# An 8192 x 8192 fp32 transpose re-tiled: two strips of 4096 columns, staggered 1024-row regions, one DMA queue

## The chip, the cores and the metric

The kernel runs on one core of one Trainium2 chip; the chip's other cores are idle. The metric is the device time of one execution in microseconds (us). All times below are medians of several executions, all of them fast. A ratio is the mean time of one kernel's fast runs over that of the other's of the same rounds, so not quite the ratio of the medians that are quoted. One caution: the profiled execution is a single one. For the kernel before it took 1276.94 us, 1.5 us more than its median.

## The reference

```python
x = np.random.randn(8192, 8192).astype(np.float32)
def reference(x):
    return np.transpose(x)
```

268.4 MB must be read and 268.4 MB written. TensorE transposes blocks of 128 x 128 from SBUF to PSUM, ScalarE (ACT) and VectorE (DVE) copy them to SBUF, and DMAs do the rest.

## The kernel before

The input is cut into 32 blocks of 1024 rows x 2048 columns. A block is loaded by two DMAs of 4 MB (packets of 8 KB, one row's piece), then transposed in 16 groups of 8 blocks of 128 x 128; each group is copied by ACT or DVE in turn, and after four groups ACT issues a store of 2 MB (4 KB contiguous in DRAM, 16 KB contiguous in SBUF). Loads go through SP's queue, stores through ACT's.

```python
R = 8; C = 16; I = R * P; J = C * P       # block: 1024 rows, 2048 columns
G = 4; LS = 2; NIN = 2; NOUT = 4; NPS = 4
# ... cut: allocation, semaphores, identity
for k, (bi, bj) in enumerate(blocks):
    # ... cut
    if k >= NIN:
        nc.sync.wait_ge(s_pe, (k - NIN + 1) * C)
    for s in range(LS):
        src = x[i0 + s * rs * P:i0 + (s + 1) * rs * P, j0:j0 + J]
        nc.sync.dma_start(out=in_tile[:, s * rs:(s + 1) * rs, :],
            in_=src.rearrange("(a p) j -> p a j", p=P)).then_inc(s_ld[slot][s], 16)
    for g in range(C // G):
        for bb in range(G):
            # ... cut: 8 transposes into one PSUM tile, a copy by ACT or DVE
        dst = out[j0 + g * G * P:j0 + (g + 1) * G * P, i0:i0 + I]
        # ... cut: ACT waits for the four copies
        if ng < NG:
            st = wide_dma(nc, nc.scalar, "qActDynamicHW", dst, outs[ob])
```

Note that the transposes of a group span all 1024 rows: no store can start before a whole block has landed.

Of the kernel before, what the change touches and what calls it, by code (L numbers as in the profile page):

```python
# [1 line left out]

# [5 lines left out]


def physical(ap):  # L10


    t = ap.tensor
    dims = [list(d) for d in ap.ap]
    if len(dims) == 2:
        dims.insert(1, [dims[1][1], 1])
    return mybir.PhysicalAccessPattern(
        ap=dims,
        offset=ap.offset,
        dtype=ap.dtype,  # L20
        memref=t.name,
        memsetref=t.name + "_set",
    )


def wide_dma(nc, eng, queue, out, in_):


    return eng.add_instruction(  # L29
        mybir.InstDMACopy(  # L30
            mode="Copy",
            name=nc.get_next_instruction_name(),
            engine=eng.engine,
            ins=[physical(in_)],
            outs=[physical(out)],
            queue=queue,
        )
    )


@with_exitstack
def kernel(
    ctx: ExitStack,
    tc: tile.TileContext,
    x: bass.AP,
    out: bass.AP,
):
    nc = tc.nc
    P = 128
    N, M = x.shape  # L50
    assert x.shape == out.shape[::-1]
    dt = x.dtype

    R = 8
    C = 16
    I = R * P
    J = C * P
    G = 4
    LS = 2
    NIN = 2  # L60
    NOUT = 4
    NPS = 4

    with tc.tile_critical():  # L64
        nc.alloc_sbuf_tensor("pad", [P, 32], dt)
        ident = nc.alloc_sbuf_tensor("ident", [P, P], dt).ap()
        ins = [nc.alloc_sbuf_tensor(f"in_tile{k}", [P, R, J], dt).ap() for k in range(NIN)]
        outs = [nc.alloc_sbuf_tensor(f"out_tile{k}", [P, G * I], dt).ap() for k in range(NOUT)]
        pss = [nc.alloc_psum_tensor(f"ps{k}", [P, I], dt).ap() for k in range(NPS)]

        s_id = nc.alloc_semaphore("s_id")
        s_ld = [[nc.alloc_semaphore(f"s_ld{k}_{s}") for s in range(LS)] for k in range(NIN)]
        s_st = [nc.alloc_semaphore(f"s_st{k}") for k in range(NOUT)]
        s_pe = nc.alloc_semaphore("s_pe")
        s_cp = [nc.alloc_semaphore("s_cpa"), nc.alloc_semaphore("s_cpv")]

        nc.gpsimd.memset(ident, 0.0).then_inc(s_id, 1)  # L77
        nc.gpsimd.wait_ge(s_id, 1)
        nc.gpsimd.affine_select(  # L79
            out=ident,  # L80
            in_=ident,
            compare_op=mybir.AluOpType.not_equal,
            fill=1.0,
            base=0,
            pattern=[[-1, P]],
            channel_multiplier=1,
        ).then_inc(s_id, 1)
        nc.tensor.wait_ge(s_id, 2)

        blocks = [(bi, bj) for bj in range(M // J) for bi in range(N // I)]  # L90
        rs = R // LS
        n = 0
        ng = 0
        NG = len(blocks) * (C // G)
        for k, (bi, bj) in enumerate(blocks):
            slot, use = k % NIN, k // NIN
            i0, j0 = bi * I, bj * J
            in_tile = ins[slot]


            if k >= NIN:
                nc.sync.wait_ge(s_pe, (k - NIN + 1) * C)
            for s in range(LS):
                src = x[i0 + s * rs * P:i0 + (s + 1) * rs * P, j0:j0 + J]
                nc.sync.dma_start(  # L105
                    out=in_tile[:, s * rs:(s + 1) * rs, :],
                    in_=src.rearrange("(a p) j -> p a j", p=P),
                ).then_inc(s_ld[slot][s], 16)
            for g in range(C // G):
                ob, ouse = ng % NOUT, ng // NOUT  # L110
                ng += 1
                for bb in range(G):
                    b = g * G + bb
                    ps = pss[n % NPS]
                    e = n % 2
                    eng = (nc.scalar, nc.vector)[e]
                    if n >= NPS:
                        nc.tensor.wait_ge(s_cp[(n - NPS) % 2], (n - NPS) // 2 + 1)
                    for a in range(R):
                        if b == 0 and a % rs == 0:  # L120
                            nc.tensor.wait_ge(s_ld[slot][a // rs], 16 * (use + 1))
                        ins_t = nc.tensor.transpose(  # L122
                            ps[:, a * P:(a + 1) * P],
                            in_tile[:, a, b * P:(b + 1) * P],
                            ident,
                        )
                    ins_t.then_inc(s_pe, 1)
                    eng.wait_ge(s_pe, n + 1)
                    if bb < 2 and ouse > 0:
                        eng.wait_ge(s_st[ob], 16 * ouse)  # L130
                    o = outs[ob][:, bb * I:(bb + 1) * I]
                    if e == 0:
                        c = nc.scalar.copy(out=o, in_=ps)  # L133
                    else:
                        c = nc.vector.tensor_copy(out=o, in_=ps)  # L135
                    c.then_inc(s_cp[e], 1)
                    n += 1
                dst = out[j0 + g * G * P:j0 + (g + 1) * G * P, i0:i0 + I]
                nc.scalar.wait_ge(s_cp[0], n // 2)
                nc.scalar.wait_ge(s_cp[1], n // 2)  # L140
                dst = dst.rearrange("(b q) i -> q b i", q=P)
                if ng < NG:
                    st = wide_dma(nc, nc.scalar, "qActDynamicHW", dst, outs[ob])
                else:
                    st = nc.scalar.dma_start(out=dst, in_=outs[ob])
                st.then_inc(s_st[ob], 16)
        for ob in range(NOUT):
            nc.sync.wait_ge(s_st[ob], 16 * (ng // NOUT))


# [1 line left out]
_INS = ['x']  # L152
_OUTS = [((8192, 8192), 'float32')]


# [23 lines left out]
```

## Time and profile before

| | before |
|---|---|
| time | 1275.41 us (1275.17 to 1275.65, 3 runs) |
| bytes moved by the kernel | 536.9 MB |
| rate between the edges (slices 3 to 38 of 40) | 425 to 430 GB/s, one slice 421 |
| load packet of 8 KB / store packet of 16 KB, most frequent duration | 309 / 615 ns |

From the page of the kernel before: the busy time of PE, the mean busy share of the 16 DMA engines in tenths in 40 slices of 31.9 us each, what they moved, and the two queues (q1 loads, q10 stores: packets, MB, share of 16 engines' time).

```profile
PE 524.8 (41%) x4096; PEld 513.3 (40%) x4096; DVE 313.5 (25%) x256; ACT 251.3 (20%) x257; POOL 0.7 (0%) x6
...
DMA  9999999999999999999999999999999999999996
GB/s 393 417 430 426 426 427 428 428 430 426 429 425 428 429 427 430 426 426 430 427 427 429 427 429 425 428 421 426 429 427 428 425 426 429 428 427 428 427 398 269
...
q1 hardware_dynamic: 33792, 268.44, 49.9%
q10 hardware_dynamic: 18816, 268.44, 49.6%
```

The DMA engines are full in all slices but the last; PE is busy for 41%. The view of waits (engine and line, what it waited for: us in total, times, longest) says the same from the other side: everybody waits for loads.

```profile
ACT out_tile L133 <- PE ps L122: 1007.6, 160, 29.6
DVE out_tile L135 <- PE ps L122: 947.2, 256, 30.4
PE ps L122 <- DMA in_tile<-in_x_dram: 734.1, 43, 26.2
```

The windows view shows the edges. Columns: the window in us, its length, busy us of each engine (with instructions), granted TensorE clock, mean busy share of the DMA engines, GB/s.

```profile
core 0: us, PE busy (x) PEld busy (x) DVE busy (x) ACT busy (x) POOL busy (x), PEclk, DMA share, GB/s
5.00:28.00 23.00, 6.39 (x40) 6.02 (x41) 1.89 (x2) 2.02 (x2) 0.00 (x0) 1.00 1.01 429
1212.00:1230.00 18.00, 10.39 (x96) 10.15 (x93) 8.09 (x7) 5.79 (x6) 0.00 (x0) 0.91 1.02 432
1230.00:1244.00 14.00, 0.00 (x0) 0.00 (x0) 0.00 (x0) 0.00 (x0) 0.00 (x0) 0.50 0.79 336
1244.00:1250.00 6.00, 5.99 (x40) 5.99 (x41) 2.26 (x2) 2.03 (x2) 0.00 (x0) 0.72 0.05 19
1250.00:1254.00 4.00, 4.00 (x39) 4.00 (x37) 2.63 (x3) 1.93 (x2) 0.00 (x0) 1.00 0.70 299
1254.00:1258.00 4.00, 4.00 (x39) 4.00 (x38) 2.76 (x3) 2.02 (x3) 0.00 (x0) 1.00 0.99 414
1272.00:1275.00 3.00, 0.00 (x0) 0.00 (x0) 0.00 (x0) 0.00 (x0) 0.00 (x0) 0.50 0.02 10
```

The first line is the start, in which only the load queue runs: one queue alone streams at about 429 GB/s. From 1230 us on, the stream falls apart: the last loads land at different times on different engines, then the last block must be transposed, and until the first of its four stores is under way the engines stand idle. In the records of the single DMA packets I counted, for each us, how much of 16 busy engines is missing. For this tail the sum is **9.9 us of full stream**. In the middle of it lie 4.9 us (4.87) in which no data packet at all is in flight. I call the first the hole's mean area, the second the standstill of all engines.

### The profile page before, as it was taken

To read this page: it belongs to the slowest core of one execution; us is meant where nothing else is said; L and a number is where in the kernel's file an instruction comes from. 1 tells how busy PE (TensorE), PEld (TensorE's weight loads), DVE (VectorE), ACT (ScalarE), POOL (GpSimd) and SP (SyncE) were. 2 spreads that over 40 slices of the span, in tenths; PEclk is the share of its full clock that TensorE was granted. 3 is DMA by queue.
4 is the path that set the end of the run, shared out by engine and by line. 5 is a ranking of instruction groups with operands and counts; after the bars stand their busy time and mean duration, and the time that the engine had idled before them with its cause. 6 is when DMAs were issued, how large, how long until landed. Compare 5 with 4: busy or idle time off the path is not lost.

```text
span 1275.1 us, 9369 instructions
## 1 busy us (share of the span) xinstructions
PE 524.8 (41%) x4096; PEld 513.3 (40%) x4096; DVE 313.5 (25%) x256; ACT 251.3 (20%) x257; POOL 0.7 (0%) x6
## 2 busy tenths in 40 slices
PE   3245523345333553425544154431454324544134
PEld 3244523345332553425544154431454314444134
DVE  1133312233112331213322133211333113332023
ACT  1122211222111221212212022211222112221112
POOL 0000000000000000000000000000000000000000
PEclk9677756777667776667766677666777667776677
DMA  9999999999999999999999999999999999999996
GB/s 393 417 430 426 426 427 428 428 430 426 429 425 428 429 427 430 426 426 430 427 427 429 427 429 425 428 421 426 429 427 428 425 426 429 428 427 428 427 398 269
DMA packets 52648, 537.47 MB, mean 421 GB/s; under 512 B 3072, under 2 KB 3072, under 8 KB 3584
## 3 DMA queue, kind: packets, MB, share of 16 engines
q1 hardware_dynamic: 33792, 268.44, 49.9%
q10 hardware_dynamic: 18816, 268.44, 49.6%
q8 instruction: 32, 0.52, 0.2%
q14 instruction: 8, 0.07, 0.0%
HBM read 268.44 MB, written 268.44 MB: 421 GB/s over the span
## 4 chain that ended last, share of the span: by engine, by line
another core or an unknown queue 39%; DMA 32%; PE 28%; issue 0%; DVE 0%; ACT 0%; ACTq 0%; SPq 0%
DMA in_tile<-in_x_dram 32%; PE ps L122 28%; DVE out_tile L135 0%; ACT out_tile L133 0%; ACTq L29 0%; SPq L105 0%; SPq L174 0%; ACTq L130 0%; ACTq L140 0%; SPq L64 0%
## 5 line engine op out<-in xcount | busy, mean ns | idle before, releaser
L122 PE MATMUL ps<-ident,in_tile 128*128 128x128 f32 x4096 | 524.8, 296 | 734.6 <-DMA in_tile<-in_x_dram 734.1
L122 PEld LDWEIGHTS ps<-ident,in_tile 128*128 128x128 f32 x4096 | 513.3, 155 | 745.8 <-DMA in_tile<-in_x_dram 702.4
L135 DVE COPY out_tile<-ps 128x1024 f32<-128x1024 f32 x256 | 313.5, 1225 | 947.2 <-PE ps L122 947.2
L133 ACT COPY out_tile<-ps 128x1024 f32<-128x1024 f32 x256 | 250.0, 1016 | 1007.6 <-PE ps L122 1007.6
L133 ACT ACT_TABLE_LOAD x1 | 1.3, 1283 | 0.9 <-SPq L64 0.9
L79 POOL TENSOR_SCALAR_AFFINE_SELECT ident<-ident 128x128 f32<-128x128 f32 x1 | 0.3, 294 | 0.2 <-POOL ident L77 0.2
L77 POOL MEMSET ident<- 128x128 f32 x1 | 0.2, 206 | 0.5 <-SPq L64 0.5
L163 POOL MEMSET const-bfloat16-1.0<- 128x1 bf16 x1 | 0.1, 102 | 0.0
L163 POOL MEMSET const-uint8-127<- 128x1 uint8 x1 | 0.1, 102 | 0.0
L163 POOL MEMSET const-float32-0.0<- 128x1 f32 x1 | 0.1, 99 | 0.2 <-issue 0.2
L163 POOL MEMSET const-float32-1.0<- 128x1 f32 x1 | 0.1, 99 | 0.0
## 6 DMA issues: line engine op xcount, KB each, us to landing
in_tile<-in_x_dram SPq DMA_DIRECT2D x64, 4096.0 KB, 39.3
out_dram<-out_tile ACTq DMA_DIRECT2D x128, 2048.0 KB, 17.6
```

The lines of the kernel that those rows point to most:

```text
L77: nc.gpsimd.memset(ident, 0.0).then_inc(s_id, 1)
L79: nc.gpsimd.affine_select(out=ident, in_=ident, compare_op=mybir.AluOpType.not_equal, fill=1.0, base=0, pattern=[[-1, P]], channel_multipl ...
L122: ins_t = nc.tensor.transpose(ps[:, a * P:(a + 1) * P], in_tile[:, a, b * P:(b + 1) * P], ident,)
L133: c = nc.scalar.copy(out=o, in_=ps)
L135: c = nc.vector.tensor_copy(out=o, in_=ps)
L163: nc = _bacc.Bacc("TRN2", target_bir_lowering=False, num_devices=1)
```

## The change

The intent: smaller steps, so that the stream never waits for a block. A strip is 4096 columns wide and is read in chunks of 128 rows (2 MB, packets of 16 KB). Its eight column ranges of 512 columns each fill a region of their own; each region takes 1024 rows, but the regions are staggered, so that one of the eight is complete and stored after each chunk. At both ends of a strip the regions are shorter (a staircase of 1 to 7 chunks). SP issues loads and stores, in one queue. The copies become half as wide and twice as many.

```diff
-    R = 8
-    C = 16
-    I = R * P
-    J = C * P
-    G = 4
-    LS = 2
-    NIN = 2
-    NOUT = 4
-    NPS = 4
+    S = 32
+    B = 4
+    W = 8
+    NR = S // B
+    NIN = 3
+    NREG = 9
+    NPS = 8
+    CH = N // P
+    J = S * P
 ... (allocation and semaphores cut)
+        for t, (s, c) in enumerate(chunks):
+            nc.tensor.wait_ge(s_ld[t % NIN], 16 * (t // NIN + 1))
+            closing = []
+            for q in [(c + k) % NR for k in range(NR)]:
+                if q not in window:
+                    end = min(c + (q - c) % W, CH - 1)
+                    r = free.pop(0)
+                    window[q] = (c, end, r)
+                    if stored[r]:
+                        (nc.scalar, nc.vector)[q % 2].wait_ge(s_st[r], 16 * stored[r])
 ... (4 transposes into one PSUM bank, one copy into the region, cut)
+                if c == end:
+                    closing.append((q, e, copied[e]))
+            for q, e, count in closing:
 ... (cut)
+                nc.sync.wait_ge(s_cp[e], count)
+                if stores:
+                    st = wide_dma(nc, nc.sync, "qSPDynamicHW", dst, regs[r][:, :B * rows])
 ... (cut)
+            if t + NIN < len(chunks):
+                nc.sync.wait_ge(s_pe, n)
+                load(t + NIN)
```

More of the change, by code (lines that the diff above doesn't have):

```diff
@@ L5 @@
 from concourse import bass_utils, mybir
-from concourse.masks import make_identity
 from concourse._compat import with_exitstack
@@ L66 @@
         ident = nc.alloc_sbuf_tensor("ident", [P, P], dt).ap()
-        ins = [nc.alloc_sbuf_tensor(f"in_tile{k}", [P, R, J], dt).ap() for k in range(NIN)]
-        outs = [nc.alloc_sbuf_tensor(f"out_tile{k}", [P, G * I], dt).ap() for k in range(NOUT)]
-        pss = [nc.alloc_psum_tensor(f"ps{k}", [P, I], dt).ap() for k in range(NPS)]
+        ins = [nc.alloc_sbuf_tensor(f"in{k}", [P, J], dt).ap() for k in range(NIN)]
+        regs = [nc.alloc_sbuf_tensor(f"reg{k}", [P, B * W * P], dt).ap() for k in range(NREG)]
+        pss = [nc.alloc_psum_tensor(f"ps{k}", [P, B * P], dt).ap() for k in range(NPS)]
         s_id = nc.alloc_semaphore("s_id")
-        s_ld = [[nc.alloc_semaphore(f"s_ld{k}_{s}") for s in range(LS)] for k in range(NIN)]
-        s_st = [nc.alloc_semaphore(f"s_st{k}") for k in range(NOUT)]
+        s_ld = [nc.alloc_semaphore(f"s_ld{k}") for k in range(NIN)]
+        s_st = [nc.alloc_semaphore(f"s_st{k}") for k in range(NREG)]
         s_pe = nc.alloc_semaphore("s_pe")
@@ L88 @@
         nc.tensor.wait_ge(s_id, 2)
-        blocks = [(bi, bj) for bj in range(M // J) for bi in range(N // I)]
-        rs = R // LS
-        n = 0
-        ng = 0
-        NG = len(blocks) * (C // G)
-        for k, (bi, bj) in enumerate(blocks):
-            slot, use = k % NIN, k // NIN
-            i0, j0 = bi * I, bj * J
-            in_tile = ins[slot]
-            if k >= NIN:
-                nc.sync.wait_ge(s_pe, (k - NIN + 1) * C)
-            for s in range(LS):
-                src = x[i0 + s * rs * P:i0 + (s + 1) * rs * P, j0:j0 + J]
-                nc.sync.dma_start(
-                    out=in_tile[:, s * rs:(s + 1) * rs, :],
-                    in_=src.rearrange("(a p) j -> p a j", p=P),
-                ).then_inc(s_ld[slot][s], 16)
-            for g in range(C // G):
-                ob, ouse = ng % NOUT, ng // NOUT
-                ng += 1
-                for bb in range(G):
-                    b = g * G + bb
-                    ps = pss[n % NPS]
-                    e = n % 2
-                    eng = (nc.scalar, nc.vector)[e]
-                    if n >= NPS:
-                        nc.tensor.wait_ge(s_cp[(n - NPS) % 2], (n - NPS) // 2 + 1)
-                    for a in range(R):
-                        if b == 0 and a % rs == 0:
-                            nc.tensor.wait_ge(s_ld[slot][a // rs], 16 * (use + 1))
-                        ins_t = nc.tensor.transpose(
-                            ps[:, a * P:(a + 1) * P],
-                            in_tile[:, a, b * P:(b + 1) * P],
-                            ident,
-                        )
-                    ins_t.then_inc(s_pe, 1)
-                    eng.wait_ge(s_pe, n + 1)
-                    if bb < 2 and ouse > 0:
-                        eng.wait_ge(s_st[ob], 16 * ouse)
-                    o = outs[ob][:, bb * I:(bb + 1) * I]
-                    if e == 0:
-                        c = nc.scalar.copy(out=o, in_=ps)
-                    else:
-                        c = nc.vector.tensor_copy(out=o, in_=ps)
-                    c.then_inc(s_cp[e], 1)
-                    n += 1
-                dst = out[j0 + g * G * P:j0 + (g + 1) * G * P, i0:i0 + I]
-                nc.scalar.wait_ge(s_cp[0], n // 2)
-                nc.scalar.wait_ge(s_cp[1], n // 2)
@@ new lines, with load @@
+        chunks = [(s, c) for s in range(M // J) for c in range(CH)]
+        def load(t):
+            s, c = chunks[t]
+            nc.sync.dma_start(
+                out=ins[t % NIN], in_=x[c * P:(c + 1) * P, s * J:(s + 1) * J]
+            ).then_inc(s_ld[t % NIN], 16)
+        for t in range(NIN):
+            load(t)
+        n = 0
+        copied = [0, 0]
+        bank = [None] * NPS
+        free = list(range(NREG))
+        stored = [0] * NREG
+        window = {}
+        stores = 0
+        for t, (s, c) in enumerate(chunks):
[8 more added lines that the diff above has]
+                        (nc.scalar, nc.vector)[q % 2].wait_ge(s_st[r], 16 * stored[r])
+                c0, end, r = window[q]
+                rows = (end - c0 + 1) * P
+                view = regs[r][:, :B * rows].rearrange("p (b i) -> p b i", b=B)
+                ps = pss[n % NPS]
+                e = q % 2
+                if bank[n % NPS] is not None:
+                    nc.tensor.wait_ge(*bank[n % NPS])
+                for b in range(B):
+                    last = nc.tensor.transpose(
+                        ps[:, b * P:(b + 1) * P],
+                        ins[t % NIN][:, (q * B + b) * P:(q * B + b + 1) * P],
+                        ident,
+                    )
+                last.then_inc(s_pe, 1)
+                n += 1
+                o = view[:, :, (c - c0) * P:(c - c0 + 1) * P]
+                i = ps.rearrange("p (b i) -> p b i", b=B)
+                (nc.scalar, nc.vector)[e].wait_ge(s_pe, n)
+                if e == 0:
+                    cp = nc.scalar.copy(out=o, in_=i)
+                else:
+                    cp = nc.vector.tensor_copy(out=o, in_=i)
+                cp.then_inc(s_cp[e], 1)
+                copied[e] += 1
+                bank[(n - 1) % NPS] = (s_cp[e], copied[e])
+                if c == end:
+                    closing.append((q, e, copied[e]))
+            for q, e, count in closing:
+                c0, end, r = window.pop(q)
+                rows = (end - c0 + 1) * P
+                j0 = s * J + q * B * P
+                dst = out[j0:j0 + B * P, c0 * P:c0 * P + rows]
@@ L141 @@
                 dst = dst.rearrange("(b q) i -> q b i", q=P)
-                if ng < NG:
-                    st = wide_dma(nc, nc.scalar, "qActDynamicHW", dst, outs[ob])
-                else:
-                    st = nc.scalar.dma_start(out=dst, in_=outs[ob])
-                st.then_inc(s_st[ob], 16)
-        for ob in range(NOUT):
-            nc.sync.wait_ge(s_st[ob], 16 * (ng // NOUT))
+                nc.sync.wait_ge(s_cp[e], count)
+                if stores:
+                    st = wide_dma(nc, nc.sync, "qSPDynamicHW", dst, regs[r][:, :B * rows])
+                else:
+                    st = nc.sync.dma_start(
+                        out=dst, in_=regs[r][:, :B * rows].rearrange("q (b i) -> q b i", b=B)
+                    )
@@ L152 @@
+                st.then_inc(s_st[r], 16)
+                stores += 1
+                stored[r] += 1
+                free.append(r)
+            if t + NIN < len(chunks):
+                nc.sync.wait_ge(s_pe, n)
+                load(t + NIN)
+        for r in range(NREG):
+            nc.sync.wait_ge(s_st[r], 16 * stored[r])
 _INS = ['x']
```

## The prediction

> What bounds it now. Both queues' packets fill 49.9% + 49.6% of the 16 DMA engines' span (the page's queue part); GB/s per slice is 425 to 430 between the edges. PE (41% busy), DVE (25%) and ACT (20%) wait: PE 734 us on loads, by the waits. The kernel is a DMA stream of 536.9 MB. At 427.5 GB/s that is 1256 us; most of the other 19 us lies at the edges.
>
> Edges (windows view). Until about 2 us nothing moves. From 1230 us the DMA share falls to 0.79, after 1244 to 0.05, until 1254 it is 0.70: the last loads are late and alone, and stores wait for a 1024-row block to be transposed (3.5 us per store). In the packet records these holes are worth 9.9 us of full stream. The last 3 us are completion.
>
> What the change does.
> 1. Tail, -10 us: when the last 2 MB load lands, two full stores (10 us) are still queued behind it, and the last chunk needs only 32 transposes (4 us at the present 121 ns). Its eight closing stores hold 36 x 256 KB, 22 us. The queue should not run dry before the end.
> 2. Loads, -5 us: packets of 8 KB become 16 KB. An 8 KB load packet takes 309 ns (one starts each 305 to 306 ns per engine in the load-only start), a 16 KB store packet 611 to 615 (606 per start when stores are alone). Two of 305.5 against 606 saves 5 ns, 1024 times per engine; 8 us if the 8 to 9 ns of fixed cost that the sizes give is wholly saved.
> 3. Staircase, +1 to +4 us: 28 of 142 stores are partial (rows of 512 to 3584 bytes instead of 4096): more, shorter packets. An estimate.
> 4. Strip boundary, 0, risk +5: eight regions close at once and chunk 64 waits for them one by one. Following the queue, copies resume with about 9 us of transfers still queued.
> 5. One queue, 0, risk either way: the Trainium skill's "DMA: Bandwidth & Descriptors", section "Issuing engines are not separate DMA queues", says that all queues run on the same 16 engines and interleave. Here one queue alone already streams at about 429 GB/s (5 to 28 us). A switch between load and store within a queue is not in this trace.
> 6. Copies, 0: twice as many of half the width, an estimated 0.65 us (DVE) and 0.55 (ACT), 2.6 us per engine in a chunk of 9.8 us. PE needs 3.9 us per chunk, and would fit at half clock. The spare region's store is next in the queue: no stall.
>
> Sum: 1275.4 - 10 - 5 + 3 = 1263. The full saving on loads, and fewer slow packets (means of 310.2 and 615.8 ns exceed the usual), could give 1250. I say 1258. All of the gain is on the critical path, since the DMA engines are it.
>
> What would show it right: DMA share 9 in all slices, the last slice above 400 GB/s (now 269) and the one before above 420 (now 398); load packets near 608 ns; about 430 GB/s in the middle; 2 us at the start as now; at most a shallow dip at the strip boundary near the middle; DVE and ACT with 512 copies each, mostly waiting.
>
> What would make it wrong: a loss at each switch of direction in the one queue (256 switches of 40 ns are 10 us); a stall at the strip boundary; partial stores much slower than their bytes; or 16 KB loads faster than thought, past 2%.

## The result, and the profile after

| | before | after |
|---|---|---|
| time, same rounds | 1275.53 us (1275.17 to 1275.89, 4 runs) | 1267.42 us (1265.92 to 1268.70, 4 runs) |
| ratio | | 0.9936 (95% interval 0.9919 to 0.9953) |
| hole at the tail, mean area | 9.9 us | none |
| missing at the very end, while engines finish one by one | 1.8 us | 3.0 us |
| packets that took over 40 ns too long, their excess per engine | 4.2 us | 5.1 us |

The change gains 8.1 us where 17.4 us were predicted (1275.4 less 1258). At a threshold of 2% the two kernels count as "same"; the interval of the ratio shows that the changed one is faster all the same.

The same parts of the page after (PEclk is the granted clock in tenths):

```profile
PE 722.6 (57%) x4096; PEld 690.6 (55%) x4096; DVE 353.5 (28%) x512; ACT 300.7 (24%) x513; POOL 0.7 (0%) x6
...
PEclk8877686777776877768667777686867877777675
DMA  9999999999999999999999999999999999999998
GB/s 380 418 428 427 428 429 428 427 428 428 426 428 429 426 428 430 429 428 428 428 417 428 428 427 428 431 429 429 429 428 428 430 428 430 429 429 429 428 428 353
...
q1 hardware_dynamic: 39264, 536.89, 100.0%
```

and the wait of PE for loads:

```profile
PE ps L131 <- DMA in<-in_x_dram: 499.7, 124, 8.3
```

PE, DVE and ACT are busy for longer (PE 722.6 us for the same 4096 transposes, was 524.8), and it costs nothing: PE still waits 500 us for loads. The mean copy of 512 columns took 692 ns on DVE and 586 ns on ACT, close to the estimate. The DMA line has no dip any more, and the last slice moves 353 GB/s where it moved 269. But it does not reach the 400 that I asked for as a proof. The windows show why:

```profile
core 0: us, PE busy (x) PEld busy (x) DVE busy (x) ACT busy (x) POOL busy (x), PEclk, DMA share, GB/s
...
1230.00:1244.00 14.00, 5.94 (x32) 5.71 (x32) 2.77 (x4) 2.34 (x4) 0.00 (x0) 0.62 1.00 425
...
1250.00:1254.00 4.00, 0.00 (x0) 0.00 (x0) 0.00 (x0) 0.00 (x0) 0.00 (x0) 0.50 0.99 415
...
1256.00:1258.00 2.00, 0.00 (x0) 0.00 (x0) 0.00 (x0) 0.00 (x0) 0.00 (x0) 0.50 0.94 377
1258.00:1260.00 2.00, 0.00 (x0) 0.00 (x0) 0.00 (x0) 0.00 (x0) 0.00 (x0) 0.50 0.60 241
1260.00:1262.00 2.00, 0.00 (x0) 0.00 (x0) 0.00 (x0) 0.00 (x0) 0.00 (x0) 0.50 0.43 170
1262.00:1265.00 3.00, 0.00 (x0) 0.00 (x0) 0.00 (x0) 0.00 (x0) 0.00 (x0) 0.50 0.08 31
```

The stream is full to 1256 us, through the last transposes. Then it does not stop, it frays: 0.94, 0.60, 0.43, 0.08. The 16 DMA engines reach the end of their work at different times. The last store's semaphore is raised by each engine as its part lands; its 16 landings are spread over 5.9 us. The Trainium skill says on "DMA: Bandwidth & Descriptors", section "Why a DMA increments its semaphore by 16 and not by 1", that a DMA runs on up to 16 engines that finish independently; this trace agrees, with 5.9 us between the first and the last. In the first microseconds of the program the spread of a load's landings is 0.3 us, so it grew over the run.

One more thing differs from the plan. At the strip boundary the eight stores took SP 30.7 us to issue, because single issues were held up for 3 to 8 us (five of the eight), and the next load was issued behind them:

```profile
605.11 30.73 SPq L28 DMA_DIRECT2D out_dram<-reg  x8
635.88 3.66 SPq L98 DMA_DIRECT2D in<-in_x_dram  x1
```

The DMA share stays at 1.00 in this stretch, so in this execution it cost nothing that the mean of the engines shows; the slice around it shows 417 instead of 428 GB/s.

### The profile page after: what moved, and what is told of

The parts are those of the page before. It is cut to its first block, busy times and chain, and to the rows that moved or that the text cites. A ratio compares the mean times of both kernels' runs of the same rounds, so it can differ in the third digit from the quotient of the medians.

```text
span 1265.1 us, 9814 instructions
## 1 busy us (share of the span) xinstructions
PE 722.6 (57%) x4096; PEld 690.6 (55%) x4096; DVE 353.5 (28%) x512; ACT 300.7 (24%) x513; POOL 0.7 (0%) x6
## 4 chain that ended last, share of the span: by engine, by line
DMA 78%; PE 20%; issue 0%; DVE 0%; ACT 0%; SPq 0%; ACTq 0%
DMA in<-in_x_dram 75%; PE ps L131 20%; DMA out_dram<-reg 2%; DVE reg L144 0%; ACT reg L142 0%; SPq L197 0%; SPq L68 0%; ACTq L140 0%
## 5 line engine op out<-in xcount | busy, mean ns | idle before, releaser
L131 PE MATMUL ps<-ident,in 128*128 128x128 f32 x4096 | 722.6, 359 | 514.8 <-DMA in<-in_x_dram 499.7
L131 PEld LDWEIGHTS ps<-ident,in 128*128 128x128 f32 x4096 | 690.6, 193 | 546.5 <-DMA in<-in_x_dram 520.8
L144 DVE COPY reg<-ps 128x512 f32<-128x512 f32 x512 | 353.5, 692 | 884.2 <-PE ps L131 850.8
L142 ACT COPY reg<-ps 128x512 f32<-128x512 f32 x512 | 299.4, 586 | 936.5 <-PE ps L131 902.7
```

The lines of the kernel that those rows point to most:

```text
L131: last = nc.tensor.transpose(ps[:, b * P:(b + 1) * P], ins[t % NIN][:, (q * B + b) * P:(q * B + b + 1) * P], ident,)
L142: cp = nc.scalar.copy(out=o, in_=i)
L144: cp = nc.vector.tensor_copy(out=o, in_=i)
```

## The experiments

Eleven kernels were run, three of them the changed kernel again, one in each job, as the base of the others. In these jobs single executions of both kernels spread over 3 to 4.5 us. The table gives medians; "before" is the kernel before in the same rounds. "Middle" is the rate in two stretches of the packet records away from the edges (100 to 560 and 750 to 1180 us after the first data), and "spread" the landings of the last store.

| run | us | before | ratio (95% interval) | middle, GB/s | spread, us |
|---|---|---|---|---|---|
| after_again | 1268.94 | 1275.68 | 0.9948 (0.9934 to 0.9961) | 428.1, 428.5 | 6.3 |
| two_queues | 1271.63 | 1275.68 | 0.9962 (0.9949 to 0.9976) | 428.5, 428.4 | 0.3 |
| load_8k | 1270.94 | 1275.68 | 0.9963 (0.9950 to 0.9975) | 426.6, 427.2 | 6.2 |
| few_instr | 1265.06 | 1275.68 | 0.9918 (0.9905 to 0.9932) | 428.7, 428.9 | 4.4 |
| base2 | 1266.13 | 1274.32 | 0.9941 (0.9929 to 0.9954) | 428.0, 428.6 | 6.1 |
| drain | 1268.58 | 1274.32 | 0.9961 (0.9947 to 0.9974) | 427.8, 428.6 | 0.2 |
| extra_end | 1267.49 | 1274.32 | 0.9948 (0.9936 to 0.9960) | 427.5, 427.6 | 5.1 |
| more_instr | 1284.67 | 1274.32 | 1.0081 (1.0068 to 1.0094) | 427.8, 427.2 | 5.9 |
| before_notail | 1267.99 | 1275.28 | 0.9944 (0.9932 to 0.9957) | 427.4, 426.5 | 5.5 |
| before_few | 1268.45 | 1275.28 | 0.9947 (0.9935 to 0.9960) | 428.4, 428.2 | 0.2 |
| base3 | 1266.76 | 1275.28 | 0.9939 (0.9924 to 0.9954) | 427.8, 428.7 | 6.5 |

The kernel before had 427.1 and 426.3 GB/s in the middle, the changed kernel's first profile 427.8 and 428.6.

The theory after the result: a hole in the stream is worth less than its mean area, because the engines do not run in step. Taking a wait away lets the difference between them stand until the end, where it has to be paid. The rivals: the tail was worth its 9.9 us, and something else took it back (switching direction in one queue, partial stores, the strip boundary).

### The changed kernel again

> The changed kernel once more, as the base for the others on this chip: 1267 us, within 1265 to 1269, 8 us below the kernel before. The 16 engines' last data should again end several us apart (5.9 us in the profile so far).

1268.94 us (1267.23 to 1270.99), with a spread of 6.3 us: as expected, with a median near the upper end. The strip boundary does show in this profile: one slice has 400 GB/s, where some engines ran out of work for a microsecond or two while another was still behind.

The two other repetitions:

> The changed kernel again, as the base of this chip: 1266 to 1270 us.

> The changed kernel again on this chip, for comparison with the two: 1266 to 1269 us, about 8 us less than the kernel before.

1266.13 and 1266.76 us; 8.2 and 8.5 us below the kernel before.

### What the tail was worth, by itself

```diff
-                for bb in range(G):
+                for bb in range(G if k < len(blocks) - 1 else 0):
```

(and SP waits for the last loads at the end). This is the kernel before, wrong in its last block: the last four stores send old buffer contents, so that they need not wait.

> The kernel before, wrong on purpose: the last block is not transposed or copied, its four stores send what the buffers hold, so they are issued before the last loads land and the hole at the tail is gone. What the hole was worth, by itself. Prediction (its mean area, 9.9 us): 9 to 10 us less than the kernel before. Theory (only the stretch in which all engines stood still, 4.9 us in the packet records, plus the little the most delayed engine waited): 5 to 7 us less, and a ragged end instead, the last landings spread over several us.

It took 1267.99 us, **7.3 us less** than the kernel before (means: 7.1). The hole of 9.9 us is gone, and in its place is the frayed end, here with a spread of 5.5 us. Windows of this run:

```profile
1230.00:1244.00 14.00, 0.00 (x0) 0.00 (x0) 0.00 (x0) 0.00 (x0) 0.00 (x0) 0.50 1.01 425
1244.00:1250.00 6.00, 0.00 (x0) 0.00 (x0) 0.00 (x0) 0.00 (x0) 0.00 (x0) 0.50 1.01 429
1250.00:1256.00 6.00, 0.00 (x0) 0.00 (x0) 0.00 (x0) 0.00 (x0) 0.00 (x0) 0.50 0.99 421
1256.00:1260.00 4.00, 0.00 (x0) 0.00 (x0) 0.00 (x0) 0.00 (x0) 0.00 (x0) 0.50 0.90 375
1260.00:1264.00 4.00, 0.00 (x0) 0.00 (x0) 0.00 (x0) 0.00 (x0) 0.00 (x0) 0.50 0.45 183
```

7.3 us is above my 5 to 7 and well below 9.9. The standstill of all engines (4.9 us) is not all that the hole cost; at the end of the kernel before, one engine finishes 1.8 us after the others (landings of the last store), and 4.9 + 1.8 would be 6.7. That reading fits but is not shown. By the mean area, 1.2 us of the missing 2.6 (9.9 less 7.3) are found again at the end, where 3.0 us are missing instead of 1.8; the remaining 1.4 us may lie in the one profile of the kernel before, which was itself 1.5 us longer than its median: profile against profile the two differ by 1276.94 - 1267.99 = 8.95 us, and the areas by 9.9 - 1.2 = 8.7. What the run does show is that the tail term of the prediction, 10 us, should have been 7, and that the whole rest of the change is worth only 1.2 us: 1267.99 against 1266.76 us for the changed kernel on the same chip, with intervals that overlap.

### A hole put back

```diff
+            if t == len(chunks) - 1:
+                for r in range(NREG):
+                    nc.sync.wait_ge(s_st[r], 16 * stored[r])
             for q, e, count in closing:
```

> The changed kernel, but SP waits for all outstanding stores before it issues the last chunk's eight, so a hole is put into the stream near the end. Theory (only the last engine's standstill costs; the others' wait for it is lost at the end anyway): the hole in the packet records averages 3 us more than the last engine's own standstill of about 4 us, but the time grows only by those 4 us (completion and new issue), and the spread of the last landings falls from about 6 to under 2 us. Rival (a hole is worth its mean area, as the prediction counted): the time grows by the 7 us of the mean hole and the spread at the end stays 6.

1268.58 us, **2.5 us more** than the base on the same chip (1266.13). Windows:

```profile
1233.00:1236.00 3.00, 3.00 (x16) 3.00 (x15) 1.25 (x2) 1.05 (x2) 0.00 (x0) 0.50 0.80 339
1236.00:1239.00 3.00, 1.15 (x10) 0.91 (x8) 0.82 (x2) 1.17 (x2) 0.00 (x0) 0.97 0.52 218
1239.00:1242.00 3.00, 0.00 (x0) 0.00 (x0) 0.00 (x0) 0.00 (x0) 0.00 (x0) 0.60 0.04 16
1242.00:1245.00 3.00, 0.00 (x0) 0.00 (x0) 0.00 (x0) 0.00 (x0) 0.00 (x0) 0.50 1.06 437
1262.00:1266.00 4.00, 0.00 (x0) 0.00 (x0) 0.00 (x0) 0.00 (x0) 0.00 (x0) 0.50 0.63 246
```

The hole's mean area in the packet records is 4.8 us (7 expected), the standstill of all engines 1.8 us (4 expected), so both sizes were too large. But the relation is as the theory has it: a hole of 4.8 us cost 2.5 us, because what was missing at the end fell from 3.0 to under 0.5 us and the spread of the last landings from 6.1 to 0.2 us. The difference between the engines is paid once, either at the hole or at the end. This is the counterpart of the previous run, and together they settle that the tail term was mis-sized and that drift is a part of it.

### Load packets of 8 KB

```diff
-            nc.sync.dma_start(out=ins[t % NIN], in_=x[c * P:(c + 1) * P, s * J:(s + 1) * J]) ...
+            for h in range(2):
+                H = J // 2
+                nc.sync.dma_start(out=ins[t % NIN][:, h * H:(h + 1) * H],
+                    in_=x[c * P:(c + 1) * P, s * J + h * H:s * J + (h + 1) * H]) ...
```

> Each load cut into two DMAs of 8 KB rows, so load packets are as before the change. If the larger packets are worth what the middle of the two traces shows (428.6 against 427.5 GB/s, 3.4 ns per 16 KB pair): +3.5 us, about 1271. If worth the 5 to 8 us of the prediction: 1272 to 1275. If packet size is worth nothing and all came from the tail: 1267.

1270.94 us, 2.0 us more than the base of the same chip (1268.94). The base itself spread over 3.8 us there, so the 2 us carry an uncertainty of about 1. The middle of the trace is steadier: 426.6 and 427.2 against 428.1 and 428.5 GB/s, about 0.3%, which over some 1256 us would be 4 us. So larger load packets are worth at most 2 to 4 us, not 5 to 8. At most, because the cut also doubles the number of load DMAs: the records show 2048 more packets of 4 bytes, 9 ns each, an estimated 1.2 us per engine that is not due to the size of the data packets.

### Two queues

```diff
-                nc.sync.wait_ge(s_cp[e], count)
+                nc.scalar.wait_ge(s_cp[e], count)
-                    st = wide_dma(nc, nc.sync, "qSPDynamicHW", dst, ...)
+                    st = wide_dma(nc, nc.scalar, "qActDynamicHW", dst, ...)
```

> The changed tiling, but stores issued by ACT on its own queue. My theory (one queue is neutral, the bound is the packets' own time): 1265 to 1270 us, the middle at about 428 GB/s. Rival A (each switch between load and store within one queue costs, 256 times some 20 to 40 ns): faster than the one-queue kernel by 4 to 8 us, about 1261. Rival B (the one queue was what saved time): slower by 4 us or more, towards 1275.

1271.63 us, 2.7 us more than the base. The middle is the same (428.5 and 428.4 GB/s): switching direction within one queue costs nothing that is seen, and one queue saves nothing either. The Trainium skill's "DMA: Bandwidth & Descriptors", section "Issuing engines are not separate DMA queues", says that DMAs issued by different engines run on the same 16 DMA engines, and this run agrees: a second queue adds no rate. Of switches between load and store it says nothing. The loss is elsewhere, in the GB/s of the 40 slices:

```profile
GB/s 395 374 426 430 429 429 429 429 429 430 428 428 428 429 429 430 428 430 428 429 349 428 427 428 430 430 429 428 428 429 429 429 429 428 430 430 429 428 427 357
```

374 in the second slice and 349 at the strip boundary: there ACT, which now issues the stores, has waits for free regions ahead of them in its program (by the waits ACT waited 283.5 us for stores to land, against 33.8 in the changed kernel), and the stream runs dry. That these waits are what empties it is read from the profile, not tested. So this run tells of queues in the middle only; as a whole it also carries the order of ACT's program.

### One staircase more in each strip

```diff
-                    end = min(c + (q - c) % W, CH - 1)
+                    end = min(c + (q - c) % W, CH // 2 - 1 if c < CH // 2 else CH - 1)
```

> Windows also close at the middle of each strip (chunk 31), so there are two more staircases: 28 more partial stores. If a staircase pair costs what the packets' sizes and durations say (2.4 us for the present 28) plus slower neighbours: +2.5 to +4 us. If the prediction's low end: +1. If closing stalls the stream (a ring full of small stores): +5 or more, with DMA holes at about 320 and 950 us.

1267.49 us, 1.4 us more than the base (means: 0.8): less than I expected after the result, and the low end of the prediction's +1 to +4. The stream shows no stall worth the name at the new boundaries (under 0.1 us in all in the packet records). 28 partial stores more cost about one microsecond, which is less than the spread of single executions.

### Fewer and more instructions

Why do the engines drift apart? In the changed kernel's first profile the spread jumped by 1.1 to 1.6 us at four moments (at about 56, 364, 677 and 983 us), each within 5 us after the start of an instruction fetch; the 62 intervals between landings in which a 16 KB fetch began hold all of its growth (6.5 us, and -0.9 in the other 207). In two repetitions it is the same (6.2 and -0.4, 5.8 and 0.2), but in after_again it is not (1.3 and 4.7), so fetches are not the only cause. The page lists two queues that carry instructions (packets, MB, share), 32 packets of 16 KB among them, of about 1.0 us each.

```profile
q8 instruction: 32, 0.52, 0.2%
q14 instruction: 12, 0.10, 0.0%
```

First fewer: one of four transposes, a wrong result.

```diff
-                for b in range(B):
+                for b in range(B if n < NPS else 1):
```

> Wrong result on purpose: after the first eight groups only one of four transposes is done, so about 6100 fewer PE instructions and some 24 fewer instruction fetches on the DMA engines (32 of about 1.0 us now); data transfers unchanged. Theory (the end is set by the most delayed engine, and fetches, each landing on one engine, are a part of the delay): spread of the last landings from 5.9 to about 3 to 4 us, 1263 to 1265 us. Rival (fetches only cost their mean, 1.5 us per engine; the spread comes from something else): 1265.5, spread still near 6. Rival (fetches are harmless): 1267.

```profile
PE 256.3 (20%) x1048; PEld 203.7 (16%) x1048; DVE 323.9 (26%) x512; ACT 270.3 (21%) x513; POOL 0.7 (0%) x6
...
GB/s 380 418 426 428 430 428 430 430 428 429 431 430 427 427 430 430 429 427 429 426 424 427 430 429 432 429 429 428 429 429 428 430 429 428 431 430 429 430 429 354
...
q8 instruction: 8, 0.13, 0.0%
```

1265.06 us, 3.9 us less than the base, and far steadier (1264.70 to 1265.36). 24 fetches less are worth 1.5 us on the mean engine; the gain is more than that, and the spread fell to 4.4 us (6.3 in the base's profile). But PE also did a quarter of its work, so this alone doesn't prove the fetches. Therefore more: the idle GpSimd sets 6144 columns of a spare tensor to zero, 48 for each chunk.

```diff
+        spare = nc.alloc_sbuf_tensor("spare", [P, 48 * 128], mybir.dt.uint8).ap()
 ...
+            nc.gpsimd.wait_ge(s_pe, n)
+            for k in range(48 * t, 48 * t + 48):
+                nc.gpsimd.memset(spare[:, k:k + 1], 0)
             if t + NIN < len(chunks):
```

> GpSimd, which is idle, does 6144 one-column memsets on a spare tensor, 48 per chunk; about 24 more instruction fetches on the DMA engines. Theory (a fetch delays one engine by about 1 us and the most delayed engine sets the end): +2 to +4 us, the opposite of the run with fewer instructions, which gained 3.9. Rival (that gain came from less PE work, not from fetches): 0 to +0.5.

It took **1284.67 us, 18.5 us more** than the base, far beyond the 2 to 4 expected. Rate in 40 slices, the instruction queues, and windows at the end:

```profile
GB/s 383 422 430 428 429 429 429 428 429 429 428 429 427 430 428 429 428 430 428 410 351 426 428 430 428 428 429 427 427 428 429 427 427 429 428 429 429 429 354 301
...
q8 instruction: 32, 0.52, 0.2%
q14 instruction: 60, 0.49, 0.1%
```

```profile
1274.00:1276.00 2.00, 0.00 (x0) 0.00 (x0) 0.00 (x0) 0.00 (x0) 0.00 (x0) 0.50 0.21 79
1276.00:1278.00 2.00, 0.00 (x0) 0.00 (x0) 0.00 (x0) 0.00 (x0) 0.00 (x0) 0.50 0.06 25
1278.00:1280.00 2.00, 0.00 (x0) 0.00 (x0) 0.00 (x0) 0.00 (x0) 0.00 (x0) 0.50 0.06 24
```

Queue 14 carries 48 packets more, of 8 KB and 0.32 us each. On the mean engine that is 48 x 0.32 / 16 = 1.0 us, on a single engine 15.4 us. From 1276 us on the DMA share is 0.06: one of 16 engines is working and 15 have finished. In the landings of the loads the last engine's distance from the last but two grows steadily, from 0.8 us at about 130 us to 6.7 us at about 590 us. At the strip boundary (351 GB/s) and at the end the others wait for it. So it is shown that a single late engine sets the time: 18.5 us, where the mean engine lost 1.0. The records don't name the engine, but the landings tell which it is: between 60 and 590 us, in the 22 intervals between successive landings that hold one of queue 14's packets of 8 KB, the last engine fell back from the last but two by another 0.48 us (median), and in the 85 intervals without one it did not (-0.01). The late engine is the one that carries these fetches, and each costs it more than the 0.32 us of the packet itself. On the Trainium skill's "Runtime: NRT & Kernel Launch", section "Instruction fetch mechanics", the sequencer drives its own DMA queue to fetch the next page, in blocks of 16 KiB, mostly hidden. Here PE's come as 16 KB packets (32 of them, 8 in the run with a quarter of the transposes), GpSimd's as 8 KB packets, and the DMA engine that carries them loses time for its other work.

The same cut in the kernel before asks whether this explains the difference between the two kernels:

```diff
-                    for a in range(R):
+                    for a in range(R if n < NPS else 2):
```

(with the wait for the second half of the load kept)

> The kernel before with one of four transposes (wrong result on purpose), so again about 24 fewer instruction fetches. If fetches delay the most delayed engine in both kernels alike: 2 to 4 us less than the kernel before, and this cost is no part of the difference between the two. If only the one-queue kernel suffers from them: 0 to -1.

1268.45 us, 6.8 us less than the kernel before, more than the 2 to 4 expected. In the packet records the standstill at the tail stayed (5.0 us, was 4.9), so the faster transposing of the last block did not shorten it. What shrank is the time in which engines finish one by one: from 5.0 to 2.0 us before the standstill and from 1.8 to under 0.2 us at the very end. Slow packets also became fewer (their excess fell by about 2 us per engine, against 0.6 us in the run of the changed kernel). So the size is confounded with whatever else less PE work changes, but the direction is the same as in the changed kernel, and the difference between the two kernels doesn't come from the number of PE's fetches (32 packets of 16 KB in each).

No experiment pointed to a correct version that beats the changed kernel: what gained (fewer transposes) isn't to be had with a right result in this program, which transposes each of its 4096 blocks of 128 x 128 once.

## Why the prediction was wrong

- **What bounds the kernel**: right. The DMA engines are the critical path before and after, and PE's 198 us of added busy time cost nothing.
- **1, the tail, "-10 us"**: the mechanism was right (the queue doesn't run dry before the end), the size was wrong. Taken away by itself the tail is worth 7.3 us. The step that failed is to book the mean area of a hole, 9.9 us, as time: the hole also absorbed difference between the engines, which now appears at the end (3.0 us missing there instead of 1.8, and 2.9 to 4.9 in the repetitions; a spread of 5.9 us). About 1.4 us of the shortfall is not located for certain.
- **2, loads, "-5 us", up to -8**: too large. Undoing it cost 2.0 us in time, and about 0.3% (4 us) by the rate in the middle, in both cases with some help of the added 4-byte packets.
- **3, staircase, "+1 to +4 us"**: right, at its low end: 28 partial stores more cost 1.4 us by the medians, 0.8 by the means (3 had been put into the sum).
- **4, strip boundary, "0, risk +5"**: right as far as the first profile shows (DMA share 1.00), though by luck: SP was held up 30.7 us in issuing, and in a second profile the slice fell to 400 GB/s.
- **5, one queue, "0"**: right; the middle is the same with two.
- **6, copies, "0"**: right, though PE took about 6.5 us for the 32 transposes of a chunk (chain of the profile), not 3.9; that still fits into the 9.8 us.
- **The step from the sum to the number**: "The full saving on loads, and fewer slow packets ... could give 1250. I say 1258." This failed altogether. Slow packets did not become fewer (excess 5.1 us per engine, was 4.2), and the full saving on loads did not come. It took 5 us off a sum of 1263 without a measured cause.

With the measured terms the books close: -7.3 (tail) - 2.0 (loads) + 1.4 (staircase) = -7.9 us, against 8.1 measured in the first comparison (6.7, 8.2 and 8.5 in the later ones). From 1258 to 1267.4 the miss of 9.4 us is 2.7 on the tail, 3.0 on the loads, 5 on the last step, less 1.6 on the staircase, together 9.1. The terms come from different jobs and each is good to about 1 us, so this sum is a check, not a proof.

## What to carry to other kernels

When a kernel is bound by DMA, do not count a hole in the stream by its mean area alone: take off what will be missing at the end in its place. Here 9.9 us became 7.3, and in the drain run 4.8 became 2.5; the standstill of all engines (4.9 and 1.8 us) was too small a count both times. Measure a hole by removing the wait with wrong data, as above, before a rewrite. Removing a point where all engines wait for each other moves their drift to the end, so part of the gain can be given back there. And don't improve on a sum of costed terms by hoping that small losses will vanish too.

## What the Trainium skill lacked or had wrong

- "Runtime: NRT & Kernel Launch" calls the cost of instruction fetches mostly hidden. For a DMA-bound kernel it lacks that they take DMA engine time on few engines: 48 fetches of 0.32 us for a GpSimd that was otherwise idle went with 18.5 us more of total time, and one engine alone was last. It also gives blocks of 16 KiB; GpSimd's fetches came as single packets of 8 KB here, most of them 17 to 33 us apart.
- "DMA: Bandwidth & Descriptors" says that engines finish independently, but not that the difference accumulates while no wait brings them together: landings of one DMA were 0.3 to 0.4 us apart at the start and 5.9 to 6.5 us after 1260 us of the changed kernel.
- The same page has no measured duration of a packet of 8 KB or 16 KB: here 309 ns and 611 to 616 ns, and loads in the smaller ones went with 0.3% less rate in the middle.
- No page that I read tells that a sequencer can be held up for microseconds in issuing a DMA: eight stores, seven of them partial, took SP 30.7 us to issue, single ones up to 8.2 us, and in the kernel before one load of 4 MB took 7.1 us. What held them is not shown.
